# Column order of matmuls: stages that stream in runs of 4 to 32, and four matmul orders in the up-projection

## The chip, the cores and the metric

One core of a Trainium2 chip runs the whole kernel in one launch. The metric is device time in microseconds (us) of that core, as the median of several executions.

## The reference, cut to what matters

One decoder layer on 256 tokens of width 2048, in float32. Every matrix product below is a large projection of all tokens; the rest is small.

```
h = rms_norm(r, g_mix);  z = h @ w_in                 # 2048 -> 10240
q, k, v, c_b, c_c, c_x, g_a, g_c = split(z)           # 6 x 1024, 2 x 2048
attn = causal softmax attention of 8 heads of 128 on q, k, v (q and k normalised)
y_attn = attn @ w_attn_out                            # 1024 -> 2048
y_conv = (c_b * causal_conv3(c_c * c_x)) @ w_conv_out # 1024 -> 2048
r = r + (sigmoid(g_a) * y_attn + sigmoid(g_c) * y_conv) @ w_o
h = rms_norm(r, g_mlp)
r = r + square(relu(h @ w_up)) @ w_down               # 2048 -> 8192 -> 2048
h = rms_norm(r, g_ple)
out = r + sigmoid(h @ w_ple_gate) * (p @ w_ple_proj)
```

## The kernel before, in words

Float32 accuracy is kept by splitting every operand in two float32r parts, hi (the value rounded by a copy) and lo (the rest). `split` makes them: ScalarE copies hi (line 88), VectorE subtracts (line 89). A product then takes three partial products, hi times hi, hi times lo and lo times hi, which TensorE adds up in PSUM.

Weights come in units of 1 MB (128 partitions by 2048 columns). SyncE issues their loads into three `raw` buffers; each unit is split into two halves of 1024 columns, and there are seven buffers for hi halves and seven for lo halves (pool `wp`). Everything that follows is written in program order, and the Tile framework sets how ScalarE and VectorE interleave the splits of later units with the evacuations.

The units of the first q stage are split in contiguous pieces of 512 columns (`load_first`). Those of the gates, branch outputs and down-projection are laid out otherwise in memory: `load_rows` splits them in pieces of 512 columns too, and each piece reads `raw` in four runs of 128 columns that lie 512 apart.

There are two ways to multiply:

- `rows` (lines 143 to 158) keeps a 128-token half of x as the stationary operand and streams 512 columns of weights. For each of 16 slices k of the width and each of two token halves it issues three matmuls of 512 columns into that half's PSUM bank (lines 154, 155 and 156). It serves q, k and v (16 slices, 96 matmuls a call, two calls each), the gates, the branch outputs and the down-projection.
- `cols` (lines 178 to 187) keeps a 128 by 128 block of weights stationary and streams x. An x tile holds hi and lo of all 256 tokens side by side, 512 columns. For each slice k, `mm` issues a matmul of w_hi with both (512 columns, line 173) and one of w_lo with x hi (256 columns, line 174), which is added to the upper half of the bank. At the last k the short one goes first (line 176 then ends the group). One call is a tile of 128 output channels, 32 matmuls in one PSUM bank; `total` then adds the two halves of the bank. It serves the convolution inputs (24 tiles), `w_o`, the up-projection and the last gate.

The accumulation banks are six (`acc`). The MLP runs in four quarters q: 16 `cols` tiles of `w_up`, each evacuated by five short operations on ScalarE and VectorE (`total`, relu times the row scale, square, split) into tiles `uT`, then four `rows` calls of `w_down` that use them. Where a program line of a helper stands in a row of the trace, the tile name tells the stage: `ps_q`, `ps_k`, `ps_v`, `ps_conv`, `ps_up`, `ps_dn`.

Of the kernel before, what the change touches and what calls it, by code (L numbers as in the profile page):

```python
# [15 lines left out]
P = 128  # L16
S = 256
# [4 lines left out]
CW = 512  # L22
KU = 4
# [12 lines left out]
def hybrid_block_kernel(ctx: ExitStack, tc: tile.TileContext, ins: dict, out: bass.AP):  # L36
# [9 lines left out]
    nc = tc.nc  # L46
# [8 lines left out]
    def slot(shape, dtype, name):  # L55
        return bp.tile(shape, dtype, tag="slot", name=name)

    def bank(name):
        return acc.tile([P, CW], F32, tag="acc", name=name)
# [20 lines left out]
    def rsqrt_mean(dst, sumsq, n, k):  # L80

        nc.vector.tensor_scalar(dst, sumsq, 1.0 / n, EPS, op0=ALU.mult, op1=ALU.add)
        nc.gpsimd.tensor_tensor(dst, dst, half[:, :k], op=ALU.pow)
# [19 lines left out]
    def run_pending(n):  # L103
        for _ in range(min(n, len(pending))):
            pending.pop(0)()


    def split_half(raw, step=HALF, between=None):
        hi = wp.tile([P, HALF], F32R, tag="hi", name="w_hi")
        lo = wp.tile([P, HALF], F32R, tag="lo", name="w_lo")  # L110
        for i in range(0, HALF, step):
            if between:
                between(i // step)
            split(hi[:, i:i + step], lo[:, i:i + step], raw[:, i:i + step])
        return hi, lo

    def load_unit(w):

        raw = wp.tile([P, UNIT], F32, tag="raw", name="raw", bufs=3)
        nc.sync.dma_start(raw, w)  # L120
        return [split_half(raw[:, h * HALF:(h + 1) * HALF]) for h in range(2)]
# [18 lines left out]
            halves.append((hi, lo))  # L140
        return halves

    def rows(units, xs, name, pops=1):

        nu = len(units)
        ps = [bank(f"ps_{name}_{t}") for t in range(NT)]
        for u, load in enumerate(units):
            wt = load()
            for j in range(KU):
                k = KU * u + j  # L150
                hi, lo = (p[:, (j % 2) * CW:(j % 2 + 1) * CW] for p in wt[j // 2])
                for t in range(NT):
                    xh, xl = (xs[k][:, i, t * P:(t + 1) * P] for i in range(2))
                    nc.tensor.matmul(ps[t], xh, hi, start=k == 0, stop=False)  # L154
                    nc.tensor.matmul(ps[t], xh, lo, start=False, stop=False)  # L155
                    nc.tensor.matmul(ps[t], xl, hi, start=False, stop=k == KU * nu - 1)  # L156
            run_pending(pops)
        return ps

    def qkv(c, load=load_unit):  # L160
        return [lambda u=u: load(ins["w_qkv"][c, u]) for u in range(4)]
# [3 lines left out]
        w = ins[wname]  # L165
        return [lambda u=u: load_rows(w[n:n + 4, :, u * CW:(u + 1) * CW]) for u in us]

    def mm(ps, wt, i, x, first, last):

        wh, wl = (p[:, (i % 8) * P:(i % 8 + 1) * P] for p in wt[i // 8])  # L170
        both = x.rearrange("p a s -> p (a s)")
        if not last:
            nc.tensor.matmul(ps, wh, both, start=first, stop=False)  # L173
        nc.tensor.matmul(ps[:, S:], wl, x[:, 0, :], start=False, stop=False)  # L174
        if last:
            nc.tensor.matmul(ps, wh, both, start=False, stop=True)  # L176

    def cols(wt, xs, name, at=0, nk=16, flush=None):

        ps = bank(f"ps_{name}")  # L180
        for k in range(nk):
            if k == flush:
                run_pending(len(pending))
            mm(ps, wt, at + k, xs[k], k == 0, k == nk - 1)
        return ps

    def total(dst, ps):
        nc.scalar.activation(dst, ps[:, S:], AF.Copy)  # L188
        nc.vector.tensor_add(dst, ps[:, :S], dst)
# [33 lines left out]
    xT, st0, xraw = {}, {}, {}  # L223
# [22 lines left out]
    def x_stats():  # L246
        for u in range(8):
            pending.append(lambda u=u: square_sum(ss0, u, xraw[u]))
        pending.append(lambda: st0.update(col=rstd_columns(ss0, "mix")))
        pending.append(lambda: st0.update(row=rstd_rows(st0["col"], "mix")))  # L250


    qs, ks, vs = {}, {}, {}

    def tokens(ps, name):

        parts = []
        for t in range(NT):
            raw = slot([P, CW], F32, f"{name}_{t}")
            nc.scalar.activation(raw, ps[t], AF.Copy, scale=st0["col"][:, t:t + 1])  # L260
            parts.append(raw)
        return parts

    def qk_evac(ps, name):
        parts = tokens(ps, name)
        ssq = sm.tile([P, NT, 4], F32, tag="ssqh", name=f"ssq_{name}")
        for t in range(NT):
            junk = sm.tile([P, HD], F32, tag="junk", name="junk", bufs=1)
            for h in range(4):
                nc.scalar.activation(junk, parts[t][:, h * HD:(h + 1) * HD], AF.Square, accum_out=ssq[:, t, h:h + 1])  # L270
        rinv = sm.tile([P, NT, 4, 1], F32, tag="rinvh", name=f"rinv_{name}")
        rsqrt_mean(rinv.rearrange("p t h o -> p (t h o)"), ssq.rearrange("p t h -> p (t h)"), HD, NT * 4)
        for t in range(NT):
            heads = parts[t].rearrange("p (h d) -> p h d", d=HD)
            nc.vector.tensor_mul(heads, heads, rinv[:, t].to_broadcast([P, 4, HD]))
        return parts
# [51 lines left out]
    for c in range(2):  # L328
        if c == 0:
            ps_q = rows(qkv(0, load_first), xT, "q0")  # L330
            x_stats()
            ps_k = rows(qkv(2), xT, "k0", pops=3)
            qs[c], ks[c] = qk_evac(ps_q, "q0"), qk_evac(ps_k, "k0")
        else:
            qs[c] = qk_evac(rows(qkv(1), xT, "q1"), "q1")
            ks[c] = qk_evac(rows(qkv(3), xT, "k1"), "k1")
        vs[c] = tokens(rows(qkv(4 + c), xT, f"v{c}"), f"v{c}")
        for h in range(4 * c, 4 * c + 4):
            head(h)


    w_in = ins["w_in"]
    row0 = st0["row"]
    convT = {}
    for j in range(8):
        cc, cx, cb = temp("cc"), temp("cx"), temp("cb")
        for i, dst in ((1, cc), (2, cx), (0, cb)):
            total(dst, cols(load_unit(w_in[8 * i + j]), xT, f"conv{i}_{j}"))
            nc.vector.tensor_mul(dst, dst, row0)
            run_pending(1)  # L350
        u = sm.tile([P, S + 2], F32, tag="u", name=f"u_{j}")
        nc.gpsimd.memset(u[:, 0:2], 0.0)
        nc.vector.tensor_mul(u[:, 2:], cc, cx)
        y = temp("y")
        nc.scalar.activation(y, u[:, 2:], AF.Copy, scale=col(W_CONV + 16 + j))
        nc.vector.scalar_tensor_tensor(y, u[:, 1:S + 1], col(W_CONV + 8 + j), y, op0=ALU.mult, op1=ALU.add)
        nc.vector.scalar_tensor_tensor(y, u[:, 0:S], col(W_CONV + j), y, op0=ALU.mult, op1=ALU.add)
        nc.vector.tensor_mul(y, y, cb)
        xsplit(convT, j, y)
# [17 lines left out]
    for c in range(4):  # L377
        gates = []
        for i in range(2):
            ps = rows(tiles("w_in", 24 + 16 * i + 4 * c), xT, f"g{i}_{c}", pops=2)  # L380
# [5 lines left out]
        for i, xs in enumerate((attnT, convT)):  # L386
            ps = rows(tiles("w_branch", 4 * c, range(2 * i, 2 * i + 2)), xs, f"y{i}_{c}")
# [18 lines left out]
    hT = {}  # L406
# [20 lines left out]
    for q in range(4):  # L427
        uT = {}
        ready = []
        for n in range(16):  # L430
            ready.append(cols(load_unit(ins["w_up"][16 * q + n]), hT, f"up_{q}_{n}"))
            if q == 0 and n == 0:
                rstd1 = rstd_columns(ss1, "mlp")
                continue
            if q == 0 and n == 1:
                row1 = rstd_rows(rstd1, "mlp")
            for ps in ready:
                a = temp("a")
                total(a, ps)
                nc.vector.scalar_tensor_tensor(a, a, 0.0, row1, op0=ALU.max, op1=ALU.mult)  # L440
                nc.scalar.activation(a, a, AF.Square)
                xsplit(uT, len(uT), a)
            ready = []
        for c in range(4):
            ps = rows(tiles("w_down", 16 * q + 4 * c), uT, f"dn_{q}_{c}")
            for t in range(NT):
                if q == 0:
                    d[c, t] = slot([P, CW], F32, f"d_{c}_{t}")
                    nc.scalar.activation(d[c, t], ps[t], AF.Copy)
                else:  # L450
                    nc.vector.tensor_add(d[c, t], ps[t], d[c, t])
            if q == 3:
                for n in (4 * c, 4 * c + 2):
                    pending.append(lambda n=n, m=(d[c, 0], d[c, 1]): transposed(n, m, end_r))
# [23 lines left out]
    ready = []  # L478
    for n in range(16):
        wt = load_unit(ins["w_ple_gate"][n])  # L480
# [5 lines left out]
        else:  # L486
            proj = bank("ps_proj_15")
            for k in range(2):
                wh, wl = (p[:, (6 + k) * P:(7 + k) * P] for p in wproj)
                xh, xl = (pT[k][:, i, :] for i in range(2))  # L490
# [11 lines left out]
        ready = []  # L502
# [55 lines left out]
```

## Time and profile before

| what | value |
|---|---|
| median of 3 runs | 1471.6 us (1471.34 to 1472.44) |
| the profiled execution | 1472.05 us, of which the span from first to last instruction is 1470.1 us |
| TensorE matmul busy | 1459.7 us, 99% of the span, 7384 matmuls |
| VectorE busy | 895.6 us, 61% |
| ScalarE busy | 757.8 us, 52% |
| DMA | 278.35 MB, 189 GB/s over the span |
| mean granted TensorE clock | 0.999 |

Matmuls are pipelined, so one's recorded duration is longer than what it costs the next; its cost is the distance from its start to the next one's start. The 1.95 us between the profiled time and its span lie around the program.

### The profile page before, as it was taken

To read this page: it belongs to the slowest core of one execution; us is meant where nothing else is said; L and a number is where in the kernel's file an instruction comes from. 1 tells how busy PE (TensorE), PEld (TensorE's weight loads), DVE (VectorE), ACT (ScalarE), POOL (GpSimd) and SP (SyncE) were. 2 spreads that over 40 slices of the span, in tenths; PEclk is the share of its full clock that TensorE was granted. 3 is DMA by queue.
4 is the path that set the end of the run, shared out by engine and by line. 5 is a ranking of instruction groups with operands and counts; after the bars stand their busy time and mean duration, and the time that the engine had idled before them with its cause. 6 is when DMAs were issued, how large, how long until landed. Compare 5 with 4: busy or idle time off the path is not lost.

```text
span 1470.1 us, 18933 instructions
## 1 busy us (share of the span) xinstructions
PE 1459.7 (99%) x7384; PEld 1237.6 (84%) x7384; DVE 895.6 (61%) x1360; ACT 757.8 (52%) x1287; POOL 11.2 (1%) x27
## 2 busy tenths in 40 slices
PE   8999999999999999999999999999999999999998
PEld 6888888888888888888888888888888888888887
DVE  7555676756464547666654566555665466666775
ACT  7655555544445444445544455445554455545543
POOL 0100000000000000000000000000000000000000
PEclk9999999999999999999999999999999999999999
DMA  8644445555555565555555555555555555555551
GB/s 315 228 173 172 172 173 174 180 191 200 186 186 200 183 248 191 180 182 191 182 190 200 187 185 190 185 198 195 178 195 186 191 200 174 200 179 189 184 203 55
DMA packets 87305, 278.35 MB, mean 189 GB/s; under 512 B 5040, under 2 KB 7344, under 8 KB 69296
## 3 DMA queue, kind: packets, MB, share of 16 engines
q1 hardware_dynamic: 87072, 277.11, 54.5%
q8 instruction: 58, 0.95, 0.3%
q14 instruction: 31, 0.25, 0.0%
q10 hardware_dynamic: 144, 0.04, 0.0%
HBM read 275.03 MB, written 2.10 MB: 189 GB/s over the span
## 4 chain that ended last, share of the span: by engine, by line
PE 99%; DMA 0%; DVE 0%; ACT 0%; issue 0%
PE ps_up L173 15%; PE ps_up L174 8%; PE ps_dn L156 8%; PE ps_dn L154 8%; PE ps_dn L155 8%; PE ps_conv L173 6%; PE ps_g L156 4%; PE ps_g L154 4%; PE ps_g L155 4%; PE ps_o L173 4%; PE ps_pg L173 4%; PE ps_conv L174 3%; PE ps_o L174 2%; PE ps_pg L174 2%; PE ps_y L156 2%; PE ps_y L154 2%
## 5 line engine op out<-in xcount | busy, mean ns | idle before, releaser
L89 DVE TENSOR_TENSOR w_lo<-raw,w_hi 128x512 fp32r<-128x512 f32 (+1 forms) x748 | 647.8, 892 | 412.1 <-ACT w_hi L88 407.1
L88 ACT ACTIVATE w_hi<-raw 128x512 fp32r<-128x512 f32 (+1 forms) x748 | 568.6, 789 | 474.1 <-PE ps_dn L156 173.9
L173 PE MATMUL ps_up<-x,w_hi 128*128 128x512 f32 x960 | 341.7, 399 | 0.0
L174 PE MATMUL ps_up<-x,w_lo 128*128 128x256 f32 x1024 | 277.1, 281 | 0.0
L173 PEld LDWEIGHTS ps_up<-x,w_hi 128*128 128x128 f32 x960 | 180.4, 188 | 41.6
L154 PE MATMUL ps_dn<-w_hi,x 128*128 128x512 f32 x512 | 199.8, 390 | 0.0
L156 PE MATMUL ps_dn<-w_hi,x 128*128 128x512 f32 x512 | 199.3, 389 | 0.0
L155 PE MATMUL ps_dn<-w_lo,x 128*128 128x512 f32 x512 | 199.2, 389 | 0.0
L174 PEld LDWEIGHTS ps_up<-x,w_lo 128*128 128x128 f32 x1024 | 193.2, 189 | 6.3
L173 PE MATMUL ps_conv<-x,w_hi 128*128 128x512 f32 x360 | 129.5, 402 | 0.0
L156 PEld LDWEIGHTS ps_dn<-w_hi,x 128*128 128x128 f32 x512 | 96.1, 188 | 20.2
L155 PEld LDWEIGHTS ps_dn<-w_lo,x 128*128 128x128 f32 x512 | 96.1, 188 | 20.0
L154 PEld LDWEIGHTS ps_dn<-w_hi,x 128*128 128x128 f32 x512 | 96.1, 188 | 19.4
L174 PE MATMUL ps_conv<-x,w_lo 128*128 128x256 f32 x384 | 103.5, 280 | 0.0
L154 PE MATMUL ps_g<-w_hi,x 128*128 128x512 f32 x256 | 99.9, 390 | 0.0
L156 PE MATMUL ps_g<-w_hi,x 128*128 128x512 f32 x256 | 99.6, 389 | 0.0
L155 PE MATMUL ps_g<-w_lo,x 128*128 128x512 f32 x256 | 99.6, 389 | 0.0
L173 PE MATMUL ps_pg<-x,w_hi 128*128 128x512 f32 x240 | 85.8, 399 | 0.0
L188 ACT ACTIVATE a<-ps_up 128x256 f32<-128x256 f32 x64 | 24.6, 384 | 118.7 <-PE ps_up L176 118.7
L173 PE MATMUL ps_o<-x,w_hi 128*128 128x512 f32 x240 | 85.6, 399 | 0.0
L173 PEld LDWEIGHTS ps_conv<-x,w_hi 128*128 128x128 f32 x360 | 67.6, 188 | 15.2
L174 PEld LDWEIGHTS ps_conv<-x,w_lo 128*128 128x128 f32 x384 | 72.5, 189 | 1.4
(184 smaller groups left out, 1686.0 us busy)
## 6 DMA issues: line engine op xcount, KB each, us to landing
raw<-in_w_up_dram SPq DMA_DIRECT2D x64, 1024.0 KB, 4.9
raw<-in_w_down_dram SPq DMA_DIRECT2D x64, 1024.0 KB, 5.1
raw<-in_w_in_dram SPq DMA_DIRECT2D x56, 1024.0 KB, 5.0
raw<-in_w_qkv_dram SPq DMA_DIRECT2D x20, 1024.0 KB, 4.9
raw<-in_w_branch_dram SPq DMA_DIRECT2D x16, 1024.0 KB, 5.1
raw<-in_w_o_dram SPq DMA_DIRECT2D x16, 1024.0 KB, 4.9
raw<-in_w_ple_gate_dram SPq DMA_DIRECT2D x16, 1024.0 KB, 5.1
raw<-in_w_qkv_dram SPq DMA_DIRECT2D x16, 256.0 KB, 5.8
```

The costliest lines, as they stand in the source:

```text
L88: nc.scalar.activation(hi, src, AF.Copy)
L89: nc.vector.tensor_sub(lo, src, hi.bitcast(F32))
L154: nc.tensor.matmul(ps[t], xh, hi, start=k == 0, stop=False)
L155: nc.tensor.matmul(ps[t], xh, lo, start=False, stop=False)
L156: nc.tensor.matmul(ps[t], xl, hi, start=False, stop=k == KU * nu - 1)
L173: nc.tensor.matmul(ps, wh, both, start=first, stop=False)
L174: nc.tensor.matmul(ps[:, S:], wl, x[:, 0, :], start=False, stop=False)
L188: nc.scalar.activation(dst, ps[:, S:], AF.Copy)
```

## The change

Nothing is computed otherwise: the same products are summed into the same banks. Two things are done in another order.

First, the columns of a matmul. `woven` views 512 (or 256) columns as h equal parts and takes e columns from each part in turn, so that the moving operand is read, and the PSUM bank written, in runs of e columns that hop between halves (h is 2) or quarters (h is 4). The stages get different pairs (h, e): k of the first head group (2, 16), v of the first (2, 8), q of the second (2, 4), k of the second (2, 32), v of the second (4, 16); the convolution tiles j = 2 and 3 (2, 16), j = 4 and 5 (2, 4), j = 6 and 7 (2, 32). The first q and the tiles j = 0 and 1 stay as they are, and so do all later stages.

Second, the order of matmuls in `w_up`. Quarter 0 stays. Quarter 1 (`step=2`) takes two slices k at a time, two long matmuls and then two short ones. Quarters 2 and 3 load two units and fill two banks side by side with `cols_two`: quarter 2 in the order long, long, short, short over the two banks, quarter 3 in the order long, short of one bank, long, short of the other.

```
+    def woven(ap, h, e):
+        return ap if h == 1 else ap.rearrange("p (h j e) -> p j h e", h=h, e=e)
...
-                hi, lo = (p[:, (j % 2) * CW:(j % 2 + 1) * CW] for p in wt[j // 2])
+                hi, lo = (woven(p[:, (j % 2) * CW:(j % 2 + 1) * CW], *weave) for p in wt[j // 2])
...
+                    to = woven(ps[t], *weave)
+                    nc.tensor.matmul(to, xh, hi, start=k == 0, stop=False)
+                    nc.tensor.matmul(to, xh, lo, start=False, stop=False)
+                    nc.tensor.matmul(to, xl, hi, start=False, stop=k == KU * nu - 1)
...
+    def high(ps, wt, i, x, first=False, last=False, weave=(1, 0)):
+        w = wt[i // 8][0][:, (i % 8) * P:(i % 8 + 1) * P]
+        both = woven(x.rearrange("p a s -> p (a s)"), *weave)
+        nc.tensor.matmul(woven(ps, *weave), w, both, start=first, stop=last)
+    def low(ps, wt, i, x, weave=(1, 0)):
+        w = wt[i // 8][1][:, (i % 8) * P:(i % 8 + 1) * P]
+        nc.tensor.matmul(woven(ps[:, S:], *weave), w, woven(x[:, 0, :], *weave), start=False, stop=False)
...
+            group = range(k, k + step)
+            if k + step < nk:
+                for i in group:
+                    high(ps, wt, at + i, xs[i], i == 0, weave=weave)
+                for i in group:
+                    low(ps, wt, at + i, xs[i], weave)
...
+    def cols_two(wts, xs, name, together):
+        ps = [bank(f"ps_{name}_{i}") for i in range(2)]
+        for k in range(16):
+            last = k == 15
+            steps = [(high, 0), (high, 1), (low, 0), (low, 1)] if together else [(high, 0), (low, 0), (high, 1), (low, 1)]
+            if last:
+                steps = [(low, 0), (high, 0), (low, 1), (high, 1)]
...
-            ps_k = rows(qkv(2), xT, "k0", pops=3)
+            ps_k = rows(qkv(2), xT, "k0", pops=3, weave=(2, 16))
...
-            total(dst, cols(load_unit(w_in[8 * i + j]), xT, f"conv{i}_{j}"))
+            total(dst, cols(load_unit(w_in[8 * i + j]), xT, f"conv{i}_{j}", weave=((1, 0), (2, 16), (2, 4), (2, 32))[j // 2]))
...
-            ready.append(cols(load_unit(ins["w_up"][16 * q + n]), hT, f"up_{q}_{n}"))
+            if q < 2:
+                ready.append(cols(load_unit(ins["w_up"][16 * q + n]), hT, f"up_{q}_{n}", step=q + 1))
+            elif n % 2 == 0:
+                continue
+            else:
+                pair = [load_unit(ins["w_up"][16 * q + n - 1 + i]) for i in range(2)]
+                ready.extend(cols_two(pair, hT, f"up_{q}_{n}", q == 2))
```

What stands on TensorE at the start of quarter 1, first tile, before (`x_...` are the x tiles of successive slices k, `w_hi` and `w_lo` the split weights):

```order
L173 MATMUL ps_up_1_0_6912<-x_4693,w_hi_6904 128x512
L174 MATMUL ps_up_1_0_6912<-x_4693,w_lo_6905 128x256
L173 MATMUL ps_up_1_0_6912<-x_4741,w_hi_6904 128x512
L174 MATMUL ps_up_1_0_6912<-x_4741,w_lo_6905 128x256
L173 MATMUL ps_up_1_0_6912<-x_4790,w_hi_6904 128x512
L174 MATMUL ps_up_1_0_6912<-x_4790,w_lo_6905 128x256
```

And in the changed kernel at the same place:

```order
L177 MATMUL ps_up_1_0_6912<-x_4693,w_hi_6904 128x512
L177 MATMUL ps_up_1_0_6912<-x_4741,w_hi_6904 128x512
L182 MATMUL ps_up_1_0_6912<-x_4693,w_lo_6905 128x256
L182 MATMUL ps_up_1_0_6912<-x_4741,w_lo_6905 128x256
L177 MATMUL ps_up_1_0_6912<-x_4790,w_hi_6904 128x512
L177 MATMUL ps_up_1_0_6912<-x_4838,w_hi_6904 128x512
```

The long matmul of the second slice has moved ahead of the short one of the first; count and widths are the same.

On TensorE at the start of quarter 2 the changed kernel has two banks, `ps_up_2_1_0` and `ps_up_2_1_1`, with weights of two units (before there is one bank a tile, in the long and short order of the first piece):

```order
L177 MATMUL ps_up_2_1_0_8362<-x_4693,w_hi_8344 128x512
L177 MATMUL ps_up_2_1_1_8363<-x_4693,w_hi_8354 128x512
L182 MATMUL ps_up_2_1_0_8362<-x_4693,w_lo_8345 128x256
L182 MATMUL ps_up_2_1_1_8363<-x_4693,w_lo_8355 128x256
L177 MATMUL ps_up_2_1_0_8362<-x_4741,w_hi_8344 128x512
L177 MATMUL ps_up_2_1_1_8363<-x_4741,w_hi_8354 128x512
```

Each x tile is now streamed four times in a row, and the first halves of both units are needed from the first matmuls on. Quarter 3 differs from this in that the second and third row of each four are exchanged.

On ScalarE in quarter 2, from the first evacuation on (`a<-ps_up` is the first step of an evacuation, `w_hi<-raw` a weight split), before:

```order
L188 ACTIVATE a_8385<-ps_up_2_0_8352 128x256
L88 ACTIVATE w_hi_8548<-raw_8546 128x1024
L441 ACTIVATE a_8385<-a_8385 128x256
L88 ACTIVATE x_8390<-a_8385 128x256
L88 ACTIVATE w_hi_8552<-raw_8546 128x1024
L188 ACTIVATE a_8436<-ps_up_2_1_8403 128x256
L88 ACTIVATE w_hi_8599<-raw_8597 128x1024
L441 ACTIVATE a_8436<-a_8436 128x256
L88 ACTIVATE x_8441<-a_8436 128x256
L88 ACTIVATE w_hi_8603<-raw_8597 128x1024
```

And in the changed kernel:

```order
L88 ACTIVATE w_hi_8548<-raw_8546 128x1024
L221 ACTIVATE a_8428<-ps_up_2_1_0_8362 128x256
L88 ACTIVATE w_hi_8552<-raw_8546 128x1024
L221 ACTIVATE a_8436<-ps_up_2_1_1_8363 128x256
L480 ACTIVATE a_8428<-a_8428 128x256
L88 ACTIVATE w_hi_8558<-raw_8556 128x1024
L88 ACTIVATE x_8433<-a_8428 128x256
L480 ACTIVATE a_8436<-a_8436 128x256
L88 ACTIVATE x_8441<-a_8436 128x256
L88 ACTIVATE w_hi_8562<-raw_8556 128x1024
```

The two evacuations of a pair now stand together behind one split of the third pair, and three more splits follow between and after their steps. The order on SyncE and GpSimd is the same in both kernels.

## Rows read from the trace of the kernel before

**Rows 1.** The page: busy time by engine, and the chain that ended last.

```profile
PE 1459.7 (99%) x7384; PEld 1237.6 (84%) x7384; DVE 895.6 (61%) x1360; ACT 757.8 (52%) x1287; POOL 11.2 (1%) x27
...
PE 99%; DMA 0%; DVE 0%; ACT 0%; issue 0%
```

**Rows 2.** Timeline of TensorE in the first v stage (start us, recorded us).

```profile
53.79 0.39 PE L156 MATMUL ps_v<-w_hi,x 128*128 128x512 f32 x1
...
74.87 0.39 PE L156 MATMUL ps_v<-w_hi,x 128*128 128x512 f32 x1
```

**Rows 3.** The chain in quarter 1 of `w_up`, three tiles apart (start us, us).

```profile
842.45 0.24 PE ps_up L174 x2
...
859.41 0.24 PE ps_up L174 x2
```

**Rows 4.** Timeline of TensorE where one tile of quarter 1 follows another.

```profile
887.52 0.40 PE L174 MATMUL ps_up<-x,w_lo 128*128 128x256 f32 x2
887.76 0.40 PE L176 MATMUL ps_up<-x,w_hi 128*128 128x512 f32 x1
887.99 0.40 PE L173 MATMUL ps_up<-x,w_hi 128*128 128x512 f32 x1
888.23 0.28 PE L174 MATMUL ps_up<-x,w_lo 128*128 128x256 f32 x1
```

**Rows 5.** TensorE's groups by form (count | busy us, mean ns).

```profile
L154 PE MATMUL ps_v<-w_hi,x 128*128 128x512 f32 x64 | 25.6, 400 | 0.0
...
L176 PE MATMUL ps_conv<-x,w_hi 128*128 128x512 f32 x24 | 9.5, 397 | 0.0
```

**Rows 6.** ScalarE's and VectorE's splits from 0 to 30 us, by form.

```profile
L88 ACT ACTIVATE w_hi<-raw 128x512 fp32r<-128x512 f32 x16 | 9.9, 625 | 4.0 <-DMA raw<-in_w_qkv_dram 3.9
L89 DVE TENSOR_TENSOR w_lo<-raw,w_hi 128x512 fp32r<-128x512 f32 x16 | 10.8, 689 | 6.8 <-ACT w_hi L88 6.8
```

**Rows 7.** ScalarE and VectorE from 820 to 1003 us, by form.

```profile
L88 ACT ACTIVATE w_hi<-raw 128x512 fp32r<-128x512 f32 x64 | 36.9, 624 | 39.6 <-PE ps_dn L156 38.1 <-PE ps_up L173 1.5
L88 ACT ACTIVATE w_hi<-raw 128x1024 fp32r<-128x1024 f32 x34 | 36.0, 1058 | 20.3 <-PE ps_dn L156 13.2 <-PE ps_up L173 7.1
L88 ACT ACTIVATE x<-a 128x256 fp32r<-128x256 f32 x16 | 6.7, 418 | 0.5
L441 ACT ACTIVATE a<-a 128x256 f32<-128x256 f32 x16 | 6.7, 418 | 0.0
L188 ACT ACTIVATE a<-ps_up 128x256 f32<-128x256 f32 x16 | 6.1, 384 | 30.0 <-PE ps_up L176 30.0
...
L89 DVE TENSOR_TENSOR w_lo<-raw,w_hi 128x1024 fp32r<-128x1024 f32 x35 | 42.9, 1225 | 27.9 <-ACT w_hi L88 27.1
L89 DVE TENSOR_TENSOR w_lo<-raw,w_hi 128x512 fp32r<-128x512 f32 x64 | 41.4, 688 | 32.1 <-ACT w_hi L88 32.1
L440 DVE SCALAR_TENSOR_TENSOR a<-a,rstd_row_mlp 128x256 f32<-128x256 f32 x16 | 6.8, 425 | 0.6
L189 DVE TENSOR_TENSOR a<-ps_up,a 128x256 f32<-128x256 f32 x16 | 6.8, 425 | 17.9 <-ACT a L188 17.9
L89 DVE TENSOR_TENSOR x<-a,x 128x256 fp32r<-128x256 f32 x16 | 6.7, 419 | 0.0
```

**Rows 8.** Timeline of TensorE in the first q stage.

```profile
9.58 0.63 PE L154 MATMUL ps_q<-w_hi,x 128*128 128x512 f32 x1
10.01 0.63 PE L155 MATMUL ps_q<-w_lo,x 128*128 128x512 f32 x1
```

**Rows 9.** The page's DMA issues (count, KB each, us from issue to landing).

```profile
raw<-in_w_up_dram SPq DMA_DIRECT2D x64, 1024.0 KB, 4.9
```

**Rows 10.** Timeline of ScalarE before and after quarter 2 begins at 1003.3 us.

```profile
995.34 1.06 ACT L88 ACTIVATE w_hi<-raw 128x1024 fp32r<-128x1024 f32 x1 [1.66 <-PE ps_dn L156]
...
1006.20 1.06 ACT L88 ACTIVATE w_hi<-raw 128x1024 fp32r<-128x1024 f32 x1 [1.63 <-PE ps_up L173]
```

More of the change, by code (lines that the diff above doesn't have):

```diff
@@ L141, in load_rows, with rows @@
         return halves
-    def rows(units, xs, name, pops=1):
+    def woven(ap, h, e):
+        return ap if h == 1 else ap.rearrange("p (h j e) -> p j h e", h=h, e=e)
+    def rows(units, xs, name, pops=1, weave=(1, 0)):
         nu = len(units)
@@ L150, in rows @@
                 k = KU * u + j
-                hi, lo = (p[:, (j % 2) * CW:(j % 2 + 1) * CW] for p in wt[j // 2])
+                hi, lo = (woven(p[:, (j % 2) * CW:(j % 2 + 1) * CW], *weave) for p in wt[j // 2])
                 for t in range(NT):
                     xh, xl = (xs[k][:, i, t * P:(t + 1) * P] for i in range(2))
-                    nc.tensor.matmul(ps[t], xh, hi, start=k == 0, stop=False)
-                    nc.tensor.matmul(ps[t], xh, lo, start=False, stop=False)
-                    nc.tensor.matmul(ps[t], xl, hi, start=False, stop=k == KU * nu - 1)
+                    to = woven(ps[t], *weave)
+                    nc.tensor.matmul(to, xh, hi, start=k == 0, stop=False)
+                    nc.tensor.matmul(to, xh, lo, start=False, stop=False)
+                    nc.tensor.matmul(to, xl, hi, start=False, stop=k == KU * nu - 1)
             run_pending(pops)
@@ L166, in tiles @@
         return [lambda u=u: load_rows(w[n:n + 4, :, u * CW:(u + 1) * CW]) for u in us]
[L168 to L176, printed above, removed]
@@ L178, in cols @@
-    def cols(wt, xs, name, at=0, nk=16, flush=None):
+    def high(ps, wt, i, x, first=False, last=False, weave=(1, 0)):
[5 more added lines that the diff above has]
+        nc.tensor.matmul(woven(ps[:, S:], *weave), w, woven(x[:, 0, :], *weave), start=False, stop=False)
@@ L180, in cols @@
+    def cols(wt, xs, name, at=0, nk=16, flush=None, weave=(1, 0), step=1):
         ps = bank(f"ps_{name}")
-        for k in range(nk):
+        for k in range(0, nk, step):
             if k == flush:
                 run_pending(len(pending))
-            mm(ps, wt, at + k, xs[k], k == 0, k == nk - 1)
+            group = range(k, k + step)
[5 more added lines that the diff above has]
+            else:
+                for i in group[:-1]:
+                    high(ps, wt, at + i, xs[i], weave=weave)
+                for i in group:
+                    low(ps, wt, at + i, xs[i], weave)
+                high(ps, wt, at + group[-1], xs[group[-1]], last=True, weave=weave)
+        return ps
@@ new lines, in cols_two @@
+    def cols_two(wts, xs, name, together):
[5 more added lines that the diff above has]
+                steps = [(low, 0), (high, 0), (low, 1), (high, 1)]
+            for f, i in steps:
+                if f is high:
+                    high(ps[i], wts[i], k, xs[k], k == 0, last)
+                else:
+                    low(ps[i], wts[i], k, xs[k])
@@ L331, in hybrid_block_kernel @@
             x_stats()
-            ps_k = rows(qkv(2), xT, "k0", pops=3)
+            ps_k = rows(qkv(2), xT, "k0", pops=3, weave=(2, 16))
             qs[c], ks[c] = qk_evac(ps_q, "q0"), qk_evac(ps_k, "k0")
         else:
-            qs[c] = qk_evac(rows(qkv(1), xT, "q1"), "q1")
-            ks[c] = qk_evac(rows(qkv(3), xT, "k1"), "k1")
-        vs[c] = tokens(rows(qkv(4 + c), xT, f"v{c}"), f"v{c}")
+            qs[c] = qk_evac(rows(qkv(1), xT, "q1", weave=(2, 4)), "q1")
+            ks[c] = qk_evac(rows(qkv(3), xT, "k1", weave=(2, 32)), "k1")
+        vs[c] = tokens(rows(qkv(4 + c), xT, f"v{c}", weave=(2, 8) if c == 0 else (4, 16)), f"v{c}")
         for h in range(4 * c, 4 * c + 4):
@@ L430, in hybrid_block_kernel @@
         for n in range(16):
-            ready.append(cols(load_unit(ins["w_up"][16 * q + n]), hT, f"up_{q}_{n}"))
+            if q < 2:
+                ready.append(cols(load_unit(ins["w_up"][16 * q + n]), hT, f"up_{q}_{n}", step=q + 1))
+            elif n % 2 == 0:
+                continue
+            else:
+                pair = [load_unit(ins["w_up"][16 * q + n - 1 + i]) for i in range(2)]
+                ready.extend(cols_two(pair, hT, f"up_{q}_{n}", q == 2))
             if q == 0 and n == 0:
```

## The prediction

> **What bounds the kernel now.** The page's busy line comes first. The reader is to see that TensorE's matmuls fill 99% of the span while VectorE stands at 61% and ScalarE at 52%, and that the chain that ended last is TensorE for 99%, with 0% for DMA, the other engines and issue [rows 1]. So nothing of this program is waited for but TensorE itself, and time changes where the distance from one matmul's start to the next changes, or where a new wait appears on TensorE.
>
> The timeline gives these distances. In the first v stage 93 matmuls of 512 columns lie between two starts, 53.79 and 74.87 us, so a long matmul costs 21.08 / 93 = 0.2267 us in `rows` [rows 2]. In `w_up` three tiles lie between 842.45 and 859.41 us, so a tile costs 5.653 us, and one of its 16 pairs of a long and a short matmul 0.3533 us [rows 3]. Where one tile follows another, two short matmuls stand together and take 0.24 us, 0.120 each [rows 4]. From 512 and 256 columns the price of a column is (226.7 - 120) / 256 = 0.417 ns, and some 13 ns come on top for each matmul. A pair at these prices would be 0.2267 + 0.120 = 0.3467 us; it takes 0.3533, so 6.7 ns a pair are lost in the present alternation. That is all that another order could win.
>
> **Part one: the woven columns.** Five stages of `rows` are woven (k, v, q, k, v), 96 matmuls each (the v stages hold 192 in all, 64 on each of three lines) [rows 5]: 480 x 0.2267 = 108.8 us. Of the 24 convolution tiles (one closing matmul each [rows 5]) 18 are woven: 18 x 5.653 = 101.8 us. So 210.6 us of the span are streamed in a new order; columns, matmuls and weight loads are as many as before.
>
> No matmul of the kernel before reads or writes its columns in short runs, so the price is bounded. From below: nothing. The nearest rows for that are the splits. In the first 30 us ScalarE takes 625 ns and VectorE 689 ns for 512 contiguous columns [rows 6]; in the down-projection the same operations read their source in four runs of 128, 512 columns apart, and take 624 and 688 ns [rows 7]. A hop between runs is free on both. These are other engines, slower per column, and the runs are longer than 4 to 32. From above: the slowest stream of 512 columns in the trace takes 0.43 us, in the first stage [rows 8]; if every woven column went at that rate, 210.6 us would grow by the factor 0.43 / 0.2267, by 189 us. I take the lower end, since the splits are the one place where this kernel shows hopping runs, and there they cost less than one part in five hundred. A gain I exclude but for the overhead of 13 ns a matmul, which nothing in the trace ties to column order.
>
> The Trainium skill speaks against this part. PSUM — Partial Sum Buffer, section Specifications (TRN2), says that any non-contiguous access pattern slows matmuls significantly; no matmul here shows that yet. Advanced Engine Details and Errata, section Memory Cachelines, narrows it: two neighbouring elements in PSUM and two hits on each 16-byte line in SBUF are enough, which runs of 4 float32 would satisfy. By the first sentence taken whole the sum would be the second rival below, by the narrower one it is zero, as the splits suggest.
>
> **Part two: the order in `w_up`.** Quarter 0 is untouched. In quarter 1 a tile has seven groups of long, long, short, short, and its last two slices keep the old order: 16 x 7 = 112 groups. In quarter 2 each of eight pairs of tiles has 15 groups: 120. The trace holds such a group already, at each tile border: short, short, long, long from 887.52 to 888.23 us is 0.71 us [rows 4], and its second long matmul goes to another bank, as in quarter 2. Two ordinary pairs are 2 x 0.3533 = 0.707 us. So a group costs the same within the 0.01 us to which the timeline reads. Bounds: at the prices without loss a group is 2 x 0.3467 = 0.693 us, 13 ns less, and 232 groups win 3.1 us; with the reading error against it a group is 0.72 us, and they lose 3.1 us. Quarter 3 keeps the alternation and changes the bank after each pair; the border from 887.76 to 887.99 us, 0.23 us for a long matmul with the next one in another bank [rows 4], shows no price for that. At best its 240 pairs lose their 6.7 ns, 1.6 us. I take zero for all, with -4.7 and +3.1 us as bounds.
>
> Pairing also gathers work on the other engines, at no cost as long as TensorE finds its halves ready. For two tiles, 11.3 us of TensorE, ScalarE has four splits of 1.058 and twice 0.384 + 0.418 + 0.418 us, together 6.7 us; VectorE has four of 1.225 and twice 0.425 + 0.425 + 0.419, together 7.4 us [rows 7]. Two loads of 4.9 us, even one after the other, fit as well [rows 9]. A pair holds four of the seven buffers, two of them are free at its middle, and the other three already hold most of the next pair. At the start of quarter 2 the fourth half is copied at 995.34 + 1.06 = 996.4 us, and the first split that waits for TensorE within the quarter is the eighth, at 1006.2 us [rows 10]; so both units stand split nearly 6 us before 1003.3 us. At the end of a quarter the two last tiles are evacuated together, and what waits behind them on ScalarE are splits of `w_down` units that are needed later. `w_down` needs the last tiles of x only from its 13th slice on, 72 matmuls or 16.3 us in; two evacuations are at most 2 x (1.22 + 1.27) = 5 us, with four splits between them some 10 us. Without this cover, each of the 16 pairs would stop TensorE for about one split, 1.06 + 1.23 us.
>
> **Sum.** 1472.05 us of the profiled execution + 0 + 0 + 0. The median of the runs shown is 0.45 us lower, and I forecast that: 1471.6 us, no change. By a 0.2% bound, 2.9 us, a measurement of this kernel can just be told from no change.
>
> **The rivals.**
>
> - A hop costs TensorE a little (slower). A matmul of 512 columns in runs of e has 512 / e runs. The five `rows` stages have 96 x (32 + 128 + 16 + 64 + 32) = 26,112 runs, the 18 tiles of 12,288 columns 6 x (768 + 3072 + 384) = 25,344. If each run lost the time of one column, 0.417 ns, that is 51,456 x 0.417 = 21.5 us, and 1493 us; if only the runs of 4 did, 30,720 of them, 12.8 us and 1484 us. It decides from 0.057 ns a run on, which is why a small price suffices. For it: TensorE streams a column in 0.417 ns, ScalarE in over 1 ns, so a hop that ScalarE hides need not be hidden here. Against it: the splits.
> - Short runs halve the stream, whatever their length: +189 us, about 1660 us. For it only the upper bound above.
> - The new orders win back the 6.7 ns a pair (faster). All of it gives 1467 us. It becomes a measurable gain from 60% of that on, or if weaving should also shorten the overhead. Against it: the group at the tile border shows none of it.
> - Pairs make TensorE wait: 16 times 2.3 us, 37 us, 1508 us. Against it: the sums of the cover above leave a third of the time free.
>
> **How the numbers follow.** No change: 0.58. A price per hop: 0.22, anywhere from 6 to 45 us. Half rate: 0.06. Waits of pairs: 0.03. A gain by order: 0.11. Faster by over 0.2% is the last alone, 0.11; slower is the three in the middle, 0.31. The range goes from the full gain, 1466.8, to the price of one column a run, 1493 us; above it stay half rate, most of the waits and something over a third of the prices per hop, about 0.17. The range of the likeliest alone is 1468.5 to 1474.7 us, the same 0.2%.
>
> **What would show it right or wrong.** Step one is right if the distance between starts in the woven k, q and v stages stays at 0.227 us and the 18 tiles at 5.65; a price per hop would show as a distance that grows with 512 / e, most in q of the second group and in tiles j = 4 and 5, least where e is 32. Step two is right if 16 tiles of each quarter still take 90.4 us (16 x 5.653) and no gap stands on TensorE at the pairs. What would make the forecast wrong is a stream that is sensitive to where its next column lies, which no row of before can exclude.

## The result: 0.5% slower, and where the time is in the profile after

The changed kernel takes 1479.75 us (median of 4, 1479.4 to 1480.03) against 1471.68 us of the kernel before (median of 4): ratio 1.0054, 95% interval 1.0042 to 1.0067. Forecast was no change at 1471.6 us. The profiled spans differ by 7.9 us (1478.0 and 1470.1).

The page of the changed kernel, busy time by engine and the chain that ended last, answers to [rows 1]:

```profile
PE 1467.6 (99%) x7384; PEld 1239.8 (84%) x7384; DVE 891.8 (60%) x1360; ACT 749.9 (51%) x1287; POOL 11.1 (1%) x27
...
PE 99%; DMA 0%; DVE 0%; ACT 0%; issue 0%
```

As many matmuls as before, TensorE busy 7.9 us longer, and still alone on the chain. The list of waits of TensorE holds one wait of any size, the one for the first x tile at the start (engine, line, what it waited for: us in total, times, longest):

```profile
PE ps_q L159 <- ACT x L91: 5.5, 1, 5.5
```

So no pair of tiles waits for its splits. The difference must lie between starts. The timeline of TensorE in the first v stage, woven (2, 8), answers to [rows 2] (start us, recorded us):

```profile
54.76 0.40 PE L161 MATMUL ps_v<-w_hi,x 128*128 128x512 f32 x1
...
77.39 0.41 PE L161 MATMUL ps_v<-w_hi,x 128*128 128x512 f32 x1
```

The same 93 steps take 22.63 us, 0.2433 us each, where it was 0.2267. In the q stage with the shortest runs, (2, 4), and in a convolution tile woven (2, 16):

```profile
79.89 0.41 PE L159 MATMUL ps_q<-w_hi,x 128*128 128x512 f32 x1
80.14 0.42 PE L160 MATMUL ps_q<-w_lo,x 128*128 128x512 f32 x1
80.39 0.41 PE L161 MATMUL ps_q<-w_hi,x 128*128 128x512 f32 x1
```

```profile
215.17 0.40 PE L177 MATMUL ps_conv<-x,w_hi 128*128 128x512 f32 x1
215.41 0.28 PE L182 MATMUL ps_conv<-x,w_lo 128*128 128x256 f32 x1
215.53 0.40 PE L177 MATMUL ps_conv<-x,w_hi 128*128 128x512 f32 x1
```

The first steps 0.25 us, the second 0.24 + 0.12. Quarter 1 of the up-projection went the other way. Its chain, four tiles apart, answers to [rows 3]:

```profile
852.31 0.70 PE ps_up L177 x3
...
874.71 0.70 PE ps_up L177 x3
```

22.40 / 4 = 5.600 us a tile against 5.653. Where quarter 2 begins, the groups over two banks answer to [rows 4]:

```profile
1012.25 0.62 PE L177 MATMUL ps_up<-x,w_hi 128*128 128x512 f32 x2
1012.70 0.40 PE L182 MATMUL ps_up<-x,w_lo 128*128 128x256 f32 x2
1012.93 0.63 PE L177 MATMUL ps_up<-x,w_hi 128*128 128x512 f32 x2
1013.40 0.39 PE L182 MATMUL ps_up<-x,w_lo 128*128 128x256 f32 x2
1013.63 0.63 PE L177 MATMUL ps_up<-x,w_hi 128*128 128x512 f32 x2
```

The first group of the quarter takes 0.68 us and the second 0.70, where the group at the tile border took 0.71. From the first matmul of each stage to that of the next, the whole account is:

| stage | pair | before us | after us | difference |
|---|---|---|---|---|
| k, first heads | (2, 16) | 22.96 | 24.18 | +1.22 |
| v, first heads | (2, 8) | 21.96 | 23.55 | +1.58 |
| q, second heads | (2, 4) | 23.86 | 26.04 | +2.17 |
| k, second heads | (2, 32) | 23.97 | 24.80 | +0.82 |
| v, second heads | (4, 16) | 23.97 | 24.32 | +0.35 |
| convolution | three pairs | 145.10 | 148.99 | +3.90 |
| `w_up` quarter 1 | order | 90.45 | 89.58 | -0.87 |
| `w_up` quarter 2 | order | 90.45 | 89.33 | -1.11 |
| `w_up` quarter 3 | order | 90.45 | 90.40 | -0.05 |

The woven stages lose 10.0 us, the orders win 2.0. All other stages agree within 0.15 us. The convolution's 3.90 us are a net figure: its 18 woven tiles lose 4.3 us (0.94 in runs of 16, 3.02 in runs of 4, 0.34 in runs of 32), and the six that nobody changed, j = 0 and 1, win 0.4.

### The profile page after: what moved, and what is told of

Read it like the earlier page. It is cut to its first block, busy times and chain, and to the rows that moved or that the text cites. A ratio compares the mean times of both kernels' runs of the same rounds, so it can differ in the third digit from the quotient of the medians.

```text
span 1478.0 us, 18917 instructions
## 1 busy us (share of the span) xinstructions
PE 1467.6 (99%) x7384; PEld 1239.8 (84%) x7384; DVE 891.8 (60%) x1360; ACT 749.9 (51%) x1287; POOL 11.1 (1%) x27
## 4 chain that ended last, share of the span: by engine, by line
PE 99%; DMA 0%; DVE 0%; ACT 0%; issue 0%
PE ps_up L177 16%; PE ps_up L182 8%; PE ps_dn L159 8%; PE ps_dn L160 8%; PE ps_dn L161 8%; PE ps_conv L177 6%; PE ps_pg L177 4%; PE ps_o L177 4%; PE ps_g L159 4%; PE ps_g L160 4%; PE ps_g L161 4%; PE ps_conv L182 3%; PE ps_o L182 2%; PE ps_pg L182 2%; PE ps_y L159 2%; PE ps_y L161 2%
## 5 line engine op out<-in xcount | busy, mean ns | idle before, releaser
L182 PE MATMUL ps_up<-x,w_lo 128*128 128x256 f32 x1024 | 240.9, 280 | 0.0
L177 PEld LDWEIGHTS ps_up<-x,w_hi 128*128 128x128 f32 x1024 | 174.8, 188 | 23.1
L177 PE MATMUL ps_conv<-x,w_hi 128*128 128x512 f32 x384 | 142.3, 409 | 0.0
L177 PE MATMUL ps_pg<-x,w_hi 128*128 128x512 f32 x256 | 92.0, 399 | 0.0
L177 PE MATMUL ps_o<-x,w_hi 128*128 128x512 f32 x256 | 89.5, 399 | 0.0
L177 PEld LDWEIGHTS ps_conv<-x,w_hi 128*128 128x128 f32 x384 | 72.3, 189 | 16.9
```

What stands on the lines that cost most here:

```text
L177: nc.tensor.matmul(woven(ps, *weave), w, both, start=first, stop=last)
L182: nc.tensor.matmul(woven(ps[:, S:], *weave), w, woven(x[:, 0, :], *weave), start=False, stop=False)
```

## Experiments

All kernels start from the changed one; what is not named is as in the kernel before. A call of the down-projection is 96 long matmuls; the ns given for it are the distance between starts, first to last over 95 steps, or the median between transposes where those stand among them (in the last quarter).

**1 and 2. Each half of the change alone.**

Weave only, and order only:

```
-            if q < 2:
-                ready.append(cols(load_unit(ins["w_up"][16 * q + n]), hT, f"up_{q}_{n}", step=q + 1))
...
+            ready.append(cols(load_unit(ins["w_up"][16 * q + n]), hT, f"up_{q}_{n}"))
```

```
-            ps_k = rows(qkv(2), xT, "k0", pops=3, weave=(2, 16))
+            ps_k = rows(qkv(2), xT, "k0", pops=3)
...
```

The second does the same at the other woven stages. Expected of the first and of the second:

> Only the woven columns of the changed kernel, the up-projection in its old order. Theory A (the woven columns cost, the new orders win a little, and the two are independent): the five woven k, v and q stages and the convolution take 10.0 us more than before, as in the changed kernel, and the quarters of the up-projection take 90.45 us again, so about 1481.5 us. Theory B (part of the loss comes from the paired tiles or from elsewhere): below 1479 us.

> Only the four orders of the up-projection, no woven columns. Theory A: quarters 1 and 2 take 0.9 and 1.1 us less, quarter 3 the same, so 1469.6 us, 0.13% under before. Theory B (the gain in these quarters was an effect of what ran ahead of them): 1471.6 us with quarters of 90.45 us.

Measured: weave only 1481.55 us, ratio 1.0065 (1.0049 to 1.0080); order only 1469.58 us, ratio 0.9985 (0.9976 to 0.9993), with quarters 1 to 3 at 89.58, 89.33 and 90.40 us. The stages of the table repeat it within 0.01 us. So the two halves are independent and of opposite sign: theory A.

**3. Sixteen pairs of parts and run.**

```
+    GRID = [(2, 4), (2, 8), (2, 16), (2, 32), (2, 64), (2, 128), (4, 4), ...]
...
-            ps = rows(tiles("w_down", 16 * q + 4 * c), uT, f"dn_{q}_{c}")
+            ps = rows(tiles("w_down", 16 * q + 4 * c), uT, f"dn_{q}_{c}", weave=GRID[4 * q + c])
```

> The up-projection in its old order, no weaving in the k, v, q and convolution stages, but each of the 16 calls of the down-projection woven by another pair (parts, run): 2 by 4, 8, 16, 32, 64, 128; 4 by 4, 8, 16, 32, 64; 8 by 4, 8, 16, 32; 16 by 16. Theory H (a price per hop, whatever the distance): the start-to-start distance over 226.7 ns grows with the number of runs, and parts do not matter: 2 by 16, 4 by 16 and 8 by 16 all read 240 ns. Theory D (the distance of the hop matters: halves lie 1 KB apart, quarters 512 bytes, eighths 256): at run 16 halves read 240, quarters 231, eighths about 227 to 231 ns; 2 by 4 reads 250 and 4 by 4 clearly less. Theory F (a fixed price for any woven order, at the boundary between two matmuls): 2 by 128 still reads 236 or more; by H it reads under 230.

| parts | run 4 | run 8 | run 16 | run 32 | run 64 | run 128 |
|---|---|---|---|---|---|---|
| 2 (1 KB apart) | 250 ns | 243 | 240 | 237 | 227 | 227 |
| 4 (512 bytes) | 268 | 231 | 231 | 233 | 227 | |
| 8 (256 bytes) | 278 | 254 to 259 | 239 | 236 | | |
| 16 (128 bytes) | | | 238 to 240 | | | |

Where two numbers stand, the pair was tried again in the run of experiment 6.

No theory holds as it stands. The number of parts matters, against H, but not in order of their distance, against D; and runs of 64 and more are free, against F. What does hold: a matmul that hops every 32 columns or oftener pays 5 to 51 ns, and the price does not go with the number of hops (128 hops of (2, 4) cost 23 ns, 32 hops of (2, 16) cost 13).

**4. Which side pays.**

```
-    def woven(ap, h, e):
+    def woven(ap, h, e, on=True):
...
+        return ap.rearrange("p (h j e) -> p j h e" if on else "p (j h e) -> p j h e", h=h, e=e)
...
+                    nc.vector.tensor_add(to, woven(ps[t], h, e, write), to)
```

The last line puts the columns back at the evacuation.

> As the run with the 16 pairs, but each of eight pairs is tried twice in the down-projection: once with only the moving operand read in the woven order (PSUM written straight), once with only PSUM written in it (the operand read straight); the evacuation puts the columns back. Pairs: 2 by 4, 8, 16, 32, then 4 by 4, 4 by 16, 8 by 16, 2 by 64. Theory R (the hop costs when SBUF is read): read-only calls show what the changed kernel shows (250, 243, 240, 237 ns for halves), write-only calls 226.7. Theory W (the hop costs when PSUM is written): the reverse. Theory S (each side pays part): both lie between, and the two excesses over 226.7 add up to the full one.

Two timelines of TensorE in this run: the first call reads in runs of 4 from halves and writes PSUM straight, the second reads straight and writes PSUM in those runs.

```profile
740.17 0.41 PE L160 MATMUL ps_dn<-w_hi,x 128*128 128x512 f32 x1
740.42 0.42 PE L161 MATMUL ps_dn<-w_lo,x 128*128 128x512 f32 x1
740.67 0.41 PE L162 MATMUL ps_dn<-w_hi,x 128*128 128x512 f32 x1
740.92 0.42 PE L160 MATMUL ps_dn<-w_hi,x 128*128 128x512 f32 x1
```

```profile
764.00 0.39 PE L160 MATMUL ps_dn<-w_hi,x 128*128 128x512 f32 x1
764.23 0.39 PE L161 MATMUL ps_dn<-w_lo,x 128*128 128x512 f32 x1
764.46 0.39 PE L162 MATMUL ps_dn<-w_hi,x 128*128 128x512 f32 x1
764.68 0.39 PE L160 MATMUL ps_dn<-w_hi,x 128*128 128x512 f32 x1
```

0.25 us against 0.227. Over the calls: read side 250, 243, 240 and 237 ns for halves in runs of 4, 8, 16 and 32, 268 for (4, 4), 231 for (4, 16), 239 for (8, 16) and 227 for (2, 64); PSUM side 227 ns for all eight pairs. Theory R: in `rows` the read of the moving operand in SBUF pays all of it, the write into PSUM nothing. In `cols`, and so in the convolution, the two sides were not tried apart. Against this stands the Trainium skill, PSUM — Partial Sum Buffer, section Specifications (TRN2), by which any non-contiguous pattern in PSUM slows matmuls; in runs of 4 and more it did not, and the measurement decides. The Trainium skill, Advanced Engine Details and Errata, section Memory Cachelines, asks for at least two hits on each 16-byte line of SBUF. Runs of four float32 are 16 bytes long, which by this should be enough; they paid 23 ns from halves and 41 from quarters.

**5. The distance of the hop, and shorter runs.**

```
+    def apart(p, e, gap):
+        v = p[:, 0:2 * gap].rearrange("p (h x) -> p h x", h=2)[:, :, 0:256]
+        return v.rearrange("p h (j e) -> p j h e", e=e)
```

> Read side alone, PSUM straight, in the 16 calls of the down-projection. A long matmul takes runs in turn from two blocks of 256 columns that start D columns apart, so it reads other columns of the weight tile than the reference does. Runs of 4 with D = 256, 260, 264, 272, 288, 320, 384, 512; runs of 16 with D = 256, 272, 288, 384, 512; run 8 with D = 264; runs of 2 and of 1 with D = 256. Theory P (what costs is that the two addresses fall together modulo some power of two): D = 256 and 512 read 250 ns at run 4 and 240 at run 16, and some of the distances between them come back to 227. Theory Q (any hop costs, and the distance does not matter): 250 at run 4 and 240 at run 16 for every D. Runs of 2 and 1 read over 250 ns by both.

Runs of 4 read 250, 251, 243, 242, 240, 250, 250 and 250 ns for the eight distances, runs of 16 read 240 for all five, run 8 with D = 264 reads 240. No distance is free: theory Q, but for up to 10 ns at D = 264 to 288. Runs of 2 read 333 ns. Runs of 1 read 216 ns, less than the contiguous 227, which no theory had.

**6. Runs of one and two.** The edit of experiment 4 with another grid.

> Sixteen calls of the down-projection as before, read side or PSUM side alone: read in runs of 1 from 2, 4, 8, 64 and 256 parts, read in runs of 2 from 2, 4 and 128 parts, PSUM written in runs of 2 from 2 and 128 parts and of 4 from 4, read 16 by 16, 8 by 4, 8 by 8, 4 by 4, and once more 2 by 1. Theory U (an operand that is read in runs of one element streams without the 13 ns that a contiguous one pays, and a hop costs only where runs are longer than one): runs of 1 read 216 ns for every number of parts, runs of 2 over 300. Theory V (the 216 ns of the last call in the distance run came of something else in that call): runs of 1 read 227 or more. PSUM writes read 227 by both.

The timelines of the first call (runs of 1 from 2 parts) and the second (from 4 parts):

```profile
744.74 0.38 PE L161 MATMUL ps_dn<-w_lo,x 128*128 128x512 f32 x1
744.96 0.38 PE L162 MATMUL ps_dn<-w_hi,x 128*128 128x512 f32 x1
745.17 0.38 PE L160 MATMUL ps_dn<-w_hi,x 128*128 128x512 f32 x1
745.39 0.38 PE L161 MATMUL ps_dn<-w_lo,x 128*128 128x512 f32 x1
```

```profile
764.78 0.45 PE L161 MATMUL ps_dn<-w_lo,x 128*128 128x512 f32 x1
765.07 0.45 PE L162 MATMUL ps_dn<-w_hi,x 128*128 128x512 f32 x1
765.35 0.45 PE L160 MATMUL ps_dn<-w_hi,x 128*128 128x512 f32 x1
765.63 0.45 PE L161 MATMUL ps_dn<-w_lo,x 128*128 128x512 f32 x1
```

216 ns from 2 parts, in the first and in the last call; 283 from 4, 488 from 8, 431 from 64, 453 from 256 (every second column). Runs of 2: 334 ns from 2 parts, 443 from 4, 451 from 128. PSUM in runs of 2: 227. Theory U is right for two parts only: two interleaved columns are the fast case, not single columns as such.

**7. Two interleaved streams at other distances.**

```
+        if gap <= 256:
+            return p[:, at:at + CW].rearrange("p (b h x) -> p b x h", h=2, x=gap)
```

> Read side alone, runs of one taken in turn from two blocks that start D columns apart, in the 16 calls of the down-projection, with D = 2, 4, 8, 16, 32, 64, 128, 256, then 257, 258, 260, 264, 272, 288, 384, 512; PSUM is written straight and the columns are not put back, and for D over 256 other columns are read than in the reference. Theory G (two interleaved streams are free for any D): 216 ns everywhere. Theory L (two streams are free as long as the two addresses do not fall on the same line or on lines that collide): D under some small bound, and some of the larger ones, read over 227 ns, the others 216. Theory Z (256 is special): 216 at 256 alone.

The timelines of the first call (D = 2) and the second (D = 4):

```profile
744.89 0.39 PE L172 MATMUL ps_dn<-w_hi,x 128*128 128x512 f32 x1
745.12 0.39 PE L170 MATMUL ps_dn<-w_hi,x 128*128 128x512 f32 x1
745.34 0.39 PE L171 MATMUL ps_dn<-w_lo,x 128*128 128x512 f32 x1
```

```profile
765.04 0.38 PE L172 MATMUL ps_dn<-w_hi,x 128*128 128x512 f32 x1
765.26 0.38 PE L170 MATMUL ps_dn<-w_hi,x 128*128 128x512 f32 x1
765.47 0.38 PE L171 MATMUL ps_dn<-w_lo,x 128*128 128x512 f32 x1
```

D = 2 reads 227 ns, D = 4 to 512 read 216 (217 at D = 258; the last three calls stand among transposes, median 216): theory G but for D = 2, where the four columns of each turn lie side by side. D = 2 and D = 4 have access patterns of the same form, so the form alone does not bring the gain; which columns follow each other does. Why two streams are fast and four or eight are slow stays open.

**8. Every moving operand of `rows` and `cols` in two interleaved streams.** The experiments pointed to this version:

```
+    def hop(ap):
+        return ap.rearrange("p (h j) -> p j h", h=2)
...
+    def back(ap):
+        return ap.rearrange("p (j h) -> p h j", h=2)
...
-                hi, lo = (woven(p[:, (j % 2) * CW:(j % 2 + 1) * CW], *weave) for p in wt[j // 2])
+                hi, lo = (hop(p[:, (j % 2) * CW:(j % 2 + 1) * CW]) for p in wt[j // 2])
...
+        both = x.rearrange("p a (h j) -> p a j h", h=2)
...
-        nc.vector.tensor_add(dst, ps[:, :S], dst)
+        nc.vector.tensor_add(halves(dst), back(ps[:, :S]), halves(dst))
```

> The kernel before with every moving operand read in runs of one from two halves (within hi and within lo in the tiles of 32 matmuls), PSUM written straight, and the columns put back by the evacuation's access pattern; no order changed. Theory U: a long matmul costs 216 instead of 227 ns and a short one 109 instead of 120, so the 3264 matmuls of rows win 35.6 us and 120 tiles of cols 453 ns each, 54 us: about 1382 us. Theory V: 1471 us or more. If TensorE streams faster but the hopping evacuation or the weight splits become late, waits show on TensorE and the time lies between.

Measured: 1387.84 us, ratio 0.9431 to before (0.9418 to 0.9444), 5.7% faster. The page and two timelines (down-projection, up-projection):

```profile
PE 1375.1 (99%) x7384; PEld 1231.9 (89%) x7384; DVE 893.7 (64%) x1360; ACT 756.2 (55%) x1287; POOL 11.2 (1%) x27
...
PE 99%; DMA 0%; DVE 0%; ACT 0%; issue 0%
```

```profile
900.05 0.38 PE L173 MATMUL ps_dn<-w_hi,x 128*128 128x512 f32 x1
900.27 0.38 PE L171 MATMUL ps_dn<-w_hi,x 128*128 128x512 f32 x1
900.49 0.38 PE L172 MATMUL ps_dn<-w_lo,x 128*128 128x512 f32 x1
```

```profile
839.76 0.38 PE L189 MATMUL ps_up<-x,w_hi 128*128 128x512 f32 x1
839.98 0.27 PE L194 MATMUL ps_up<-x,w_lo 128*128 128x256 f32 x1
840.09 0.38 PE L189 MATMUL ps_up<-x,w_hi 128*128 128x512 f32 x1
```

A long matmul steps 0.216 us, a pair 0.33; quarters of the up-projection take 83.84 instead of 90.45 us, those of the down-projection 82.88 instead of 87.05. TensorE is still 99% of the chain, VectorE's and ScalarE's busy times are within 0.3% of before: the hopping evacuation costs nothing that shows. Of the 6 us above the expected 1382, 4.8 lie in the 1920 pairs, which take 327.5 ns (83.84 us over 256) instead of 325.

**9. Longer groups of long and short.**

```
-                ready.append(cols(load_unit(ins["w_up"][16 * q + n]), hT, f"up_{q}_{n}", step=q + 1))
...
+            ready.append(cols(load_unit(ins["w_up"][16 * q + n]), hT, f"up_{q}_{n}", step=(2, 4, 8, 16)[q]))
```

> No woven columns. All long matmuls of a group of slices first, then its short ones: groups of 2, 4, 8 and 16 slices in quarters 0 to 3 of the up-projection, and of 1, 2, 4 and 8 slices in the convolution tiles j = 0 and 1, 2 and 3, 4 and 5, 6 and 7. Theory O (a tile loses 106 ns, 5.653 against 5.547 us at the prices without loss, and loses it by the number of times that long and short alternate): 5.600, 5.573, 5.560 and 5.553 us a tile for groups of 2, 4, 8 and 16 in the up-projection. Theory X (the group of two wins by something else, such as two short ones in a row): no further gain from 4 on, 5.60 us in all four quarters.

Quarters 1, 2 and 3, with groups of 4, 8 and 16, took 89.65, 89.37 and 89.05 us, 5.60, 5.59 and 5.57 a tile; groups of 2 in the run with the orders alone 89.58. Quarter 0, with groups of 2, took 90.88 us instead of 91.48. The convolution tiles, six with groups of 2, 4 and 8 each, took 36.68 us instead of 36.77, 36.68 instead of 36.57 and 34.73 instead of 34.98. In all 1467.94 us in a single run, against 1471.53 before. Longer groups win a little more, but groups of four no more than groups of two: neither theory fits.

The starts in quarter 3 show where the loss sits. After a change from short to long, five long matmuls step 233, 236, 229, 232 and 231 ns before 227 returns, about 28 ns in all; after the change back the first two short ones step 113 and 119 instead of 120, about 8 ns less. A change to and fro thus costs 20 ns. With one a tile (groups of 16) that makes 5.547 + 0.020 = 5.567 us, with two (groups of 8) 5.587, as measured. Groups of four change before the long ones have recovered and pay 14 ns each time, four times a tile. So the price of a change is not fixed, as theory O had it. Why TensorE takes five matmuls to recover stays open.

**10. Groups of four on top of version 8.**

```
+            ready.append(cols(load_unit(ins["w_up"][16 * q + n]), hT, f"up_{q}_{n}", step=4))
...
+        add_to_r(n, cols(load_unit(ins["w_o"][n]), mT, f"o_{n}", flush=12, step=4))
```

> The kernel with all moving operands read in runs of one, and groups of four long and then four short matmuls in all tiles of 16 slices. In the run without the groups a pair of long and short takes 327.5 ns against 216 + 109 = 325, so the alternation costs 2.5 ns. Theory O: groups of four win three quarters of it, 120 tiles x 16 x 1.9 ns = 3.6 us, 1384 us. Theory X: nothing, 1388 us.

1387.70 us, ratio 0.9429 to before (0.9416 to 0.9442): the same as version 8. Theory X; with interleaved operands the order is worth nothing.

## Why the prediction was wrong, step by step

**What bounds the kernel** was right: TensorE alone, before and after, and every difference is one of distances between starts.

**Part one, the woven columns, failed.** The step was "I take the lower end, since the splits are the one place where this kernel shows hopping runs". ScalarE's and VectorE's free hops [rows 6, 7] say nothing of what TensorE pays to read: there the term of zero was 10.0 us, 4 to 23 ns for each of the 480 long matmuls of `rows` and 3.9 us in the convolution. The splits were also the wrong length: their runs are of 128 columns, and TensorE too reads runs of 64 and 128 at 227 ns (experiment 3), so these rows could not tell the price of runs of 4 to 32. The caution stood in the first rival, that a hop which ScalarE hides need not be hidden on TensorE, and that rival was right in sign and place (in `rows` and in the convolution the runs of 4 lost most). Its size was not: one column a run made 21.5 us, measured were 10.0, since the price does not go with the number of runs: (2, 32) with 16 runs pays 10 ns, not 7, and (2, 4) with 128 pays 23, not 53. Also wrong was "a gain I exclude but for the overhead of 13 ns a matmul, which nothing in the trace ties to column order": experiments 6 to 8 tie 11 of these 13 ns to column order (226.7 against 215.8 ns).

**The bound from above**, 0.43 us a matmul from the first stage, came from rows that hop nowhere. Of the changed kernel's pairs the dearest stepped 0.25 us, and half rate did not occur; but in experiment 6 runs of one from eight parts stepped 0.488 us, so it was no bound for hopping reads as such.

**The place within part one.** The sentence of the Trainium skill's page on PSUM was weighed as the rule against this change. Slower came out, but not by it: PSUM pays nothing (experiment 4).

**Part two, the order**, was mis-sized. The term was zero, with -4.7 and +3.1 us as bounds; it measured -2.0 us in the changed kernel and -2.2 us alone (1469.58 against 1471.78). The group at the tile border, 0.71 us [rows 4], was taken for the steady one; over a whole quarter the groups save 0.87 / 112 = 7.8 ns in quarter 1 and 1.11 / 120 = 9.3 ns in quarter 2, which a timeline that reads to 10 ns could not tell. Quarter 3, zero, was right at -0.05 us.

**The cover for the paired tiles** was right: no wait of TensorE at the pairs, quarter 3 with its pairs is as long as before, and the rival of waits (37 us) did not occur.

**The sum** of the true terms, +10.0 - 2.0 us, lay inside the range of 1466.8 to 1493 us; the likeliest case was the wrong one. The range held by luck in size: its upper end was one column a run, a price that no run showed.

## What to carry to other kernels

Where TensorE streams back to back, take the distance between starts at two widths: their difference gives the price of a column, and what is left belongs to the matmul. Here most of it could be had back by the read order of the moving operand (5.7% of this kernel). A free access pattern on ScalarE or VectorE is no evidence for TensorE, nor are long runs evidence for short ones; when no row shows an operation at all, give its price and its sign an experiment of one stage per value, as a down-projection of 16 equal calls allows, and split it by side (operand read, PSUM written) before calling it free.

## What the runs showed of the hardware that was not expected

A contiguous float32r operand of 512 columns costs 226.7 ns, two interleaved streams of 256 cost 215.8, and four 283: reading straight is not the fastest order. A read of every second column costs twice as much (453 ns). PSUM written in runs of 2 to 64 columns cost 227 ns, the same as straight.

The distances lock into fixed patterns. In the run of 16 pairs, (2, 16) reads 240 ns at every step, (2, 4) alternates 246 and 254, and straight pairs of a long and a short matmul in the up-projection mostly repeat every third: 349, 350 and 361 ns. In the same run the first tile of quarter 3 alternates, from its second pair on, at 347 ns a pair, which is the price without loss. A stage that nobody changed can fall into another pattern: the three convolution tiles of j = 0 took 18.07 us instead of 18.27 in the changed kernel, those of j = 1 18.30 instead of 18.50, with the attention matmuls between them. Which pattern a stage falls into, and why, was not tried.
